# Where the modulation columns of a diffusion trunk are worked out: seven to a head of the linear attention, sixteen beside the output product, few in the up products

## The chip, the cores and the metric

The kernel runs on one core of a Trainium2 chip. The metric is the device time of one execution in microseconds (us). Engines are named as in the profile: PE is TensorE (matrix products), DVE is VectorE, ACT is ScalarE, POOL is GpSimd, and SP (SyncE) issues the DMAs.

## The reference

A diffusion trunk of two layers over 512 tokens of 1024 channels, with a context of 256 tokens:

```python
for l in range(DEPTH):                     # DEPTH = 2
    m = (silu(c) @ ada_w[l] + ada_b[l]).reshape(-1, 6, 1, 1024)      # six modulations
    h = x * (1 + m[:, 1]) + m[:, 0]
    if l % 2 == 0:
        y = even_mixer(h, hc, ...)         # SSD and HGRN2 linear attention, then w_out
    else:
        y = conformer_conv(h, ...)
    x = layer_norm(ALPHA * x + m[:, 2] * y, ...)
    h = x * (1 + m[:, 4]) + m[:, 3]
    u, g = split(h @ w_up)                 # 1024 -> 2 x 2816
    f = (gelu(conv3x3(g)) * u) @ w_down    # 2816 -> 1024
    x = layer_norm(ALPHA * x + m[:, 5] * f, ...)
```

`even_mixer` multiplies h by one wide matrix, runs a state-space scan over 16 heads and a gated linear recurrence (S = diag(f) S + k v, o = S q) over 8 heads in both directions, normalises and gates both results, and multiplies them by `w_out`. Everything is fp32.

A **modulation column** is 128 channels of one of the six modulations of one layer: 8 columns to a modulation, 48 to a layer. The layer's first two modulations of layer 0, for the latent and for the context, are worked out at the start and are 32 columns; 80 columns are left.

## The kernel before

Channels lie on the partitions and tokens along the free axis. fp32 products are made of three matmuls: each operand is split into a high and a low half (hi, lo), and a block is hi x hi + lo x hi + hi x lo (L213 to L215, or L220 to L222 with the activation as the stationary operand). Weights come in loads of four 128 x 128 blocks (256 KB, `wraw`, L181), issued on SP's queue; ACT makes the high half (`whi`, L183) and DVE or POOL the low half (`wlo`, L187): POOL at the start and from the output product on, DVE in between. Six such loads have room.

The stages with their place in the profiled execution:

- start (0 to 110 us) with 32 columns, and the state-space scan (110 to 285);
- linear attention (`gla`, 285 to 640): eight heads, two to a pair. PE makes f, q and v of a head by products of h (`ps`, `psv`, and `psz` for gates). Then seven **levels** follow one another: PE makes four score matmuls (`lev`, L730), DVE merges them into p under a mask (L732), and multiplies the keys and queries `kq` by decays `t` (L734, L736, L738), of which it halves the number for the next level (L740); ACT copies the keys (`kg`, L727). At the end of a head PE transposes keys (`pk`), ACT copies them (`kt`), PE makes `pu`, DVE the states `s` (L755), and PE the output `po`. Products for the next head stand between the levels;
- merge (640 to 682): transposes of y and o (`pt`, L799), the second half of the gate product, and `gate` (L772), which multiplies o by 1/rms (r) and by the gate (sg);
- output product (682 to 755), norm, then the feed-forward part of layer 0: up products with a 3 x 3 convolution on DVE in 22 blocks (up0, 785 to 1030; `acc`, L1021, which reads a product from PSUM, nine taps less one), down products (down0, to 1155);
- layer 1: conformer, up1 (1404 to 1633), down1, output.

A column is one DMA of 512 KB on SP's queue (`ada`, L257), one DVE instruction over 128 x 1024 elements (`junk`, L260) that sums the products of the matrix row and silu(c), and a read of the accumulator (`mod`). Nothing else uses `junk`.

`ada_some(n)` (L264) takes n columns from the list `ada_todo`. It writes them so that they are issued after the instruction in `self.after`, if there is one. The list scheduler that orders each engine's instructions is free to put them later or to move others around them. The columns before are placed so:

- 24 (layer 0, modulations 2, 4 and 3): 8 in merge, 16 behind the output product, with no instruction to come after;
- 56 (layer 0's modulation 5 and all of layer 1): one call in each of the 22 up blocks and calls of 6 in the down products. `self.after` is the last instruction of the norm before (set in `post`) in all of them, and all 56 stand in up0.

The pool `adap` has two buffers for `ada`, so that the third load waits for the first column.

Of the kernel before, what the change touches and what calls it, by code (L numbers as in the profile page):

```python
# [47 lines left out]
GRP = 3  # products that start together after a norm  # L48
NW1, NC1 = 5, 3  # products side by side where the operand comes block by block
# products before a norm that go by halves of the tokens, and for how many of them the weights stay for both halves  # L50
TAIL_W, TAIL_D, TAIL_C = (2, 1), (2, 1), (4, 2)
WB, NWB = 4, 6  # blocks of a load, and loads that have room
# [3 lines left out]
def weight_blocks():  # L56
    """The order in which 128x128 weight blocks are used: (matrix, row, column)."""
# [90 lines left out]
class Net:  # L148
# [28 lines left out]
    def _wload(self):  # L177
# [7 lines left out]
        # by GpSimd where VectorE mostly reads PSUM, which leaves it the port they share  # L185
# [4 lines left out]
    def wblock(self, expect, n=1):  # L190
        """The next n blocks, which lie side by side."""
        while ORDER[self.wpos] is None:
            self.wpos += 1
        p = self.wpos
        assert ORDER[p] == expect, (ORDER[p], expect)
        self.wpos += n
        i, j = divmod(p, WB)
        self.prefetch(i + 1 + self.LA)
        assert j + n <= WB
        hi, lo = self.wtiles[i]  # L200
        return hi[:, j * P:(j + n) * P], lo[:, j * P:(j + n) * P]

    def prefetch(self, upto=None):
        """Weight tiles up to a position, or those of the next products."""
# [5 lines left out]
    def mm3w(self, ps, w, a, start, stop):  # L210
        """ps += w^T a: the weight is the stationary operand."""
# [5 lines left out]
    def mm3a(self, ps, a, w, start, stop):  # L217
        """ps += a^T w: the activation is the stationary operand."""
# [5 lines left out]
    def fm(self, pool, w, col, act, kt=KT, tag="mm", n=T, also=None):  # L224
        """Feature-major product: psum [128 channels, n tokens] (and a second one for `also`)."""
# [14 lines left out]
    def rsqrt(self, y, v, tmp, itmp):  # L240
        """y = v ** -0.5 for small [128, n] tiles: a seed from the exponent, then Newton steps."""
# [9 lines left out]
    def ada(self, layer, j, i, cond=None, out=None, raw=None):  # L251
        """Column of modulation j, channels i*128..: sum_k ada_w[k, ch] silu(c)[k] + ada_b."""
# [6 lines left out]
        junk = self.adap.tile([P, D], BF16, tag="junk", name="junk", bufs=2)  # L259
# [48 lines left out]
    def modulated(self, x, s1, sh, hi, lo, tmp):  # L308
        """hi + lo = x * s1 + sh, split for the tensor engine."""
# [5 lines left out]
    def conv5(self, ps, n, ci, tmps, out=None):  # L315
        """silu of the 5-tap convolution along tokens of a [128, n] psum tile."""
# [12 lines left out]
    def to_tokens(self, src, dst, n, mi):  # L329
        """PE transposes of [128 ch, n*128 tok] into dst [128 tok, n, 128 ch]."""  # L330
# [6 lines left out]
    def mixer(self):  # L337
# [13 lines left out]
        # activations in token blocks as the stationary operand  # L351
# [11 lines left out]
        # startup  # L363
# [8 lines left out]
        with self.pool("pst", 1, PSUM) as pst:  # L372
# [31 lines left out]
            # context modulation, with products of the latent alone meanwhile  # L404
# [19 lines left out]
        self.ada_todo = [(0, j, i) for j in (2, 4, 3) for i in range(8)]  # L424
# [13 lines left out]
        # B of the context  # L438
# [34 lines left out]
        gd = gl.enter_context(self.pool("gla2", 2))  # L473
        for hp in range(4):
# [10 lines left out]
        # gates of the first heads, while the last head's levels follow one another  # L485
# [12 lines left out]
    def dt_stage(self, act, actc, sp, sx, mm, mi, rows):  # L498
# [19 lines left out]
        # softplus = max(x, 0) + 2 atanh(e / (2 + e)), e = exp(-|x|)  # L518
# [21 lines left out]
        # decays: inclusive up to the token, exclusive after it, whole chunks  # L540
# [19 lines left out]
    def zproj(self, i, sz, acth, pool, tag, col=C_Z, dst=None):  # L560
        """silu of 256 channels of a gate, tokens on the partitions."""
# [16 lines left out]
    def ssd(self, g, y, xct, bfm, cfm, btok, dts, rows, sz, sp, tmps, lv, mi):  # L578
# [6 lines left out]
        def bch(t, n):  # [P, GH] -> [P, GH, n] by repetition  # L585
            return bass.AP(tensor=t.tensor, offset=t.offset, ap=[list(t.ap[0]), [1, t.shape[1]], [0, n]])
# [12 lines left out]
        # states: the backward ones for every chunk, the forward one as it goes  # L599
# [12 lines left out]
        # C B^T, transposed: [source, target], cut into the two directions  # L612
# [57 lines left out]
    def gla(self, h, v, act, actc, qs, o, so, gp, gd, mm, lv, mi):  # L670
# [3 lines left out]
        kq = gd.tile([P, 4, T], F32, tag="kq", name="kq")  # K forward, K backward, Q backward, Q forward  # L674
# [13 lines left out]
        # context: keys carried to the end of the context in each direction  # L688
# [24 lines left out]
        # scores inside chunks, target along the free axis: the diagonal, then blocks of 1, 2, .. 64  # L713
# [10 lines left out]
        while m < P:  # L724
# [15 lines left out]
            TT(out=t2, in0=t[:, :, 0::2], in1=t[:, :, 1::2], op=ALU.mult)  # L740
            t, n, m, lev = t2, n // 2, m * 2, lev + 1
        # states at the chunks' starts
# [23 lines left out]

    def gate(self, o, sg, r, h, n):
        """o * r * sg for n heads from h on."""
# [5 lines left out]
    def merge(self, mx, ox, y, o, so, acth):  # L774
# [3 lines left out]
        mp = op.enter_context(self.pool("mop"))  # L778
        ohi = mp.tile([P, 16, T], F32R, name="ohi")
        olo = mp.tile([P, 16, T], F32R, name="olo")  # L780
        ps_ = self.stack()
        self.adap = op.enter_context(self.pool("adap", 2))
# [26 lines left out]
        self.ada_some(8)  # L809
# [10 lines left out]
        # the residual, times alpha, comes back in place of o and stays  # L820
# [10 lines left out]
        bk = [self.mm.tile([P, T], F32, tag="mm", name="psg") for _ in range(NW1)]  # L831
        for k in range(16):
            for i in range(NW1):
                self.mm3w(bk[i], self.wblock(("wout", k * P, i * P)), (ohi[:, k, :], olo[:, k, :]), k == 0, k == 15)
        self.ada_some(99)
# [3 lines left out]
        assert not self.ada_todo  # L839
# [3 lines left out]
        self.ada_todo = [(0, 5, i) for i in range(8)] + [(1, j, i) for j in (2, 1, 0, 4, 3, 5) for i in range(8)]  # L843
        self.post(ln, 0, 0)

# [1 line left out]
    def project(self, ln, w, act, kt, layer, j, tail, then=None, first=0):  # L847
        """x = x + gate * (W^T act), with the norm's sums; the last `tail` blocks go by halves of the tokens."""
# [328 lines left out]
```

## Time and profile before

| | us |
|---|---|
| runs | 1776.51, 1777.94, 1782.64 |
| median | 1777.94 |
| span of the profiled execution, first to last instruction | 1775.1 |
| fastest run over that span | 1.4 |
| linear attention, 285 to 640 | 355 |
| up0, first up matmul to first down matmul | 245.0 |
| up1, the same | 229.0 |

The profile is of one execution. Its span is what the sum is made against; the runs hold a little more than the span. A row of a group of instructions gives the line, engine, operation, tiles and shapes, a count, the busy time and the mean length of one in ns, and behind the last bar the time the engine was idle before them and what it waited for. A row of the timeline gives the start, the length and the same names. An engine's instructions overlap, so the start-to-start distance, not the length, is what a further instruction costs.

### The profile page before, as it was taken

To read this page: it belongs to the slowest core of one execution; us is meant where nothing else is said; L and a number is where in the kernel's file an instruction comes from. 1 tells how busy PE (TensorE), PEld (TensorE's weight loads), DVE (VectorE), ACT (ScalarE), POOL (GpSimd) and SP (SyncE) were. 2 spreads that over 40 slices of the span, in tenths; PEclk is the share of its full clock that TensorE was granted. 3 is DMA by queue.
4 is the path that set the end of the run, shared out by engine and by line. 5 is a ranking of instruction groups with operands and counts; after the bars stand their busy time and mean duration, and the time that the engine had idled before them with its cause. 6 is when DMAs were issued, how large, how long until landed. Compare 5 with 4: busy or idle time off the path is not lost.

```text
span 1775.1 us, 26151 instructions
## 1 busy us (share of the span) xinstructions
PE 1707.4 (96%) x9430; PEld 1457.2 (82%) x9430; DVE 1259.0 (71%) x2384; ACT 845.3 (48%) x1698; POOL 557.3 (31%) x436
## 2 busy tenths in 40 slices
PE   6999999999999999999999999999989999999996
PEld 4987768989999997887777888988869888888886
DVE  6778988857574785589999841478788876776125
ACT  3556775354444544373333332395655744333233
POOL 4400000000000003544566554533414444444451
PEclk9999999999999999999999999999989999999998
DMA  9721001021111147636677433322112333333331
GB/s 344 248 72 48 31 19 53 31 60 36 55 42 54 43 142 259 216 98 200 231 247 246 142 113 96 106 78 60 55 29 78 90 96 100 96 96 99 97 103 64
DMA packets 92195, 194.02 MB, mean 109 GB/s; under 512 B 10497, under 2 KB 13569, under 8 KB 92065
## 3 DMA queue, kind: packets, MB, share of 16 engines
q1 hardware_dynamic: 92016, 192.21, 34.5%
q8 instruction: 74, 1.21, 0.3%
q14 instruction: 57, 0.46, 0.1%
q0 software_dynamic: 48, 0.13, 0.0%
HBM read 190.21 MB, written 2.10 MB: 108 GB/s over the span
## 4 chain that ended last, share of the span: by engine, by line
PE 80%; DVE 15%; DMA 2%; issue 1%; ACT 1%; SPq 0%; POOL 0%; ACTq 0%; POOLq 0%; DVEq 0%
PE ps L213 15%; PE ps L215 15%; PE ps L214 15%; DVE acc L1021 4%; DVE junk L260 4%; PE lev L730 3%; PE psg L214 2%; PE psg L213 2%; PE psg L215 2%; PE psh L214 2%; PE psh L213 2%; PE psh L215 2%; PE seg L631 2%; PE psz L221 1%; PE psz L220 1%; PE psz L222 1%
## 5 line engine op out<-in xcount | busy, mean ns | idle before, releaser
L187 POOL TENSOR_TENSOR wlo<-wraw,whi 128x512 fp32r<-128x512 f32 x388 | 541.4, 1403 | 1172.3 <-ACT whi L183 1153.2
L183 ACT CAST whi<-wraw 128x512 fp32r<-128x512 f32 x488 | 298.1, 618 | 418.8 <-PE ps L214 214.5
L213 PE MATMUL ps<-h1hi,whi 128*128 128x512 f32 x760 | 297.9, 392 | 12.1 <-DVE acc L1021 12.0
L215 PE MATMUL ps<-h1hi,wlo 128*128 128x512 f32 x760 | 297.1, 391 | 0.3 <-POOL wlo L187 0.2
L214 PE MATMUL ps<-h1lo,whi 128*128 128x512 f32 x760 | 296.7, 390 | 0.0
L1021 DVE SCALAR_TENSOR_TENSOR acc<-ps,pcol,acc 128x441 f32<-128x441 f32 (+2 forms) x320 | 216.9, 691 | 34.8 <-ACT acc L1013 28.6
L213 PEld LDWEIGHTS ps<-h1hi,whi 128*128 128x128 f32 x760 | 143.1, 188 | 45.6 <-issue 16.9
L215 PEld LDWEIGHTS ps<-h1hi,wlo 128*128 128x128 f32 x760 | 143.1, 188 | 30.8 <-POOL wlo L187 1.2
L214 PEld LDWEIGHTS ps<-h1lo,whi 128*128 128x128 f32 x760 | 143.3, 188 | 29.1
L260 DVE CUSTOM_DVE_ANT_0 junk<-ada,sc,pcol 128x1024 bf16<-128x1024 f32 x80 | 113.3, 1419 | 27.4 <-DMA ada<-adaw 27.4
L872 DVE SCALAR_TENSOR_TENSOR x<-ps,mod,x 128x512 f32<-128x512 f32 x14 | 10.5, 750 | 148.9 <-PE ps L215 148.9
L187 DVE TENSOR_TENSOR wlo<-wraw,whi 128x512 fp32r<-128x512 f32 x100 | 68.9, 693 | 53.0 <-ACT whi L183 45.9
L1098 DVE SCALAR_TENSOR_TENSOR cr<-u,pcol,cr 128x256 f32<-128x256 f32 (+24 forms) x172 | 104.6, 682 | 1.4 <-ACT cr L1077 1.2
L215 PE MATMUL ps<-ghi,wlo 128*128 128x512 f32 x264 | 102.8, 389 | 0.0
L213 PE MATMUL ps<-ghi,whi 128*128 128x512 f32 x264 | 102.8, 389 | 0.0
L214 PE MATMUL ps<-glo,whi 128*128 128x512 f32 x264 | 102.8, 389 | 0.0
L213 PE MATMUL ps<-hhi,whi 128*128 128x512 f32 x240 | 98.2, 409 | 0.0
L1023 ACT ACTIVATE acc<-acc 128x512 f32<-128x512 f32 x44 | 27.7, 632 | 145.0 <-DVE acc L1021 145.0
L215 PE MATMUL ps<-hhi,wlo 128*128 128x512 f32 x240 | 96.1, 400 | 0.0
L214 PE MATMUL ps<-hlo,whi 128*128 128x512 f32 x240 | 95.8, 399 | 0.0
L939 DVE TENSOR_TENSOR glo<-acc,ghi 128x512 fp32r<-128x512 f32 x44 | 61.4, 1397 | 18.6 <-ACT ghi L938 18.4
L222 PE MATMUL psz<-whi,hlo 128*128 128x256 f32 (+1 forms) x224 | 67.6, 302 | 0.0
(366 smaller groups left out, 4167.1 us busy)
## 6 DMA issues: line engine op xcount, KB each, us to landing
wraw<-wst SPq DMA_DIRECT2D x488, 256.0 KB, 2.7
ada<-adaw SPq DMA_DIRECT2D x104, 512.0 KB, 4.1
xk<-xT SPq DMA_DIRECT2D x8, 256.0 KB, 7.8
x<-xT SPq DMA_DIRECT2D x8, 256.0 KB, 4.8
out<-n SPq DMA_DIRECT2D x16, 128.0 KB, 1.7
xk<-ctxT SPq DMA_DIRECT2D x8, 128.0 KB, 4.4
sc<-rows SPq DMA_DIRECT2D x1, 512.0 KB, 4.4
scc<-rows SPq DMA_DIRECT2D x1, 512.0 KB, 7.6
```

Source lines behind the costliest of these rows:

```text
L183: nc.scalar.copy(hi, raw)
L187: eng.tensor_tensor(out=lo, in0=raw, in1=hi.bitcast(F32), op=ALU.subtract)
L213: mm(ps, w[0], a[0], start=start, stop=False)
L214: mm(ps, w[0], a[1], start=False, stop=False)
L215: mm(ps, w[1], a[0], start=False, stop=stop)
L222: mm(ps, a[1], w[0], start=False, stop=stop)
L260: nc.vector.tensor_tensor_reduce(out=junk, in0=raw, in1=self.sc if cond is None else cond, scale=1.0, scalar=self.pc("adab", n), op0=ALU.m ...
L631: nc.tensor.matmul(seg, (self.gt, self.lt)[d], r[:, d], start=d == 0, stop=d == 1)
L730: nc.tensor.matmul(ps[:, c, :], kg[:, c * P:(c + 1) * P], ap(kq, 2 * T + c * P, [[2 * m, P // (2 * m)], [T + m, 2], [1, m]]), start=True, ...
L939: nc.vector.tensor_tensor(out=lo, in0=x, in1=hi.bitcast(F32), op=ALU.subtract)
L1021: nc.vector.scalar_tensor_tensor(out=o, in0=grid(pg)[:, r0 + dy - 1:r1 + dy - 1, c0 + dx - 1:c1 + dx - 1], scalar=wcol(dy, dx), in1=o, op0 ...
L1098: nc.vector.scalar_tensor_tensor(out=acc[:, t0:t1], in0=u[:, t0 + d:t1 + d], scalar=self.pc("cdw", tap * 8 + i), in1=acc[:, t0:t1], op0=AL ...
```

## The change

There is one list of 80 columns, and it is given out earlier. `gla` gives out one column behind each level's last multiplication (`ADA_HEAD` = 7, so at all seven levels), to be issued after that multiplication: 56 columns. 16 more (`ADA_OUT`) are asked for ahead of the output product, to be issued after the last head's last such multiplication. Eight are left for the feed-forward part of layer 0: one in every fourth up block (6, after that block's split) and 2 in the first down product. Layer 1 works out none, as before. `junk` has one buffer and not two, and `adap` is opened in the attention, and in merge ahead of `ohi`. `residual` and `split` now hand out their instruction for `self.after`. The comments are taken out, which moves line numbers by 1 to 6.

```diff
-        junk = self.adap.tile([P, D], BF16, tag="junk", name="junk", bufs=2)
+        junk = self.adap.tile([P, D], BF16, tag="junk", name="junk", bufs=1)
...
-        self.ada_todo = [(0, j, i) for j in (2, 4, 3) for i in range(8)]
+        self.ada_todo = [(l, j, i) for l, js in ((0, (2, 4, 3, 5)), (1, (2, 1, 0, 4, 3, 5))) for j in js for i in range(8)]
...
         gd = gl.enter_context(self.pool("gla2", 2))
+        self.adap = gl.enter_context(self.pool("adap", 2))
...
-            TT(out=t2, in0=t[:, :, 0::2], in1=t[:, :, 1::2], op=ALU.mult)
+            self.after = TT(out=t2, in0=t[:, :, 0::2], in1=t[:, :, 1::2], op=ALU.mult)
+            if lev < self.ADA_HEAD:
+                self.ada_some(1)
             t, n, m, lev = t2, n // 2, m * 2, lev + 1
...
+    ADA_HEAD, ADA_OUT, ADA_DOWN = 7, 16, 5
...
         mp = op.enter_context(self.pool("mop"))
+        self.adap = op.enter_context(self.pool("adap", 2))
         ohi = mp.tile([P, 16, T], F32R, name="ohi")
         olo = mp.tile([P, 16, T], F32R, name="olo")
         ps_ = self.stack()
-        self.adap = op.enter_context(self.pool("adap", 2))
...
         emit(o, "hnw", 0, 8)
-        self.ada_some(8)
...
+        self.ada_some(self.ADA_OUT)
         for k in range(16):
             for i in range(NW1):
                 self.mm3w(bk[i], self.wblock(("wout", k * P, i * P)), (ohi[:, k, :], olo[:, k, :]), k == 0, k == 15)
-        self.ada_some(99)
...
-        assert not self.ada_todo
...
-        self.ada_todo = [(0, 5, i) for i in range(8)] + [(1, j, i) for j in (2, 1, 0, 4, 3, 5) for i in range(8)]
...
-            self.split(acc, ghi[:, i, :], glo[:, i, :])
+            self.after = self.split(acc, ghi[:, i, :], glo[:, i, :])
...
-            self.ada_some(1)
+            if layer == DEPTH - 1 or i % 4 == 0:
+                self.ada_some(1)
...
-        self.project(ln, f"dn{layer}", lambda k: (ghi[:, k, :], glo[:, k, :]), FT, layer, 5, TAIL_D, lambda i: self.ada_some(6))
+        self.project(ln, f"dn{layer}", lambda k: (ghi[:, k, :], glo[:, k, :]), FT, layer, 5, TAIL_D, lambda i: self.ada_some(0 if layer or i > 3 else self.ADA_DOWN))
```

What it makes of the order is seen at three places. In rows of the order, a column is `ISA junk,mod<-ada,sc,pcol` and the `ISA mod` behind it.

DVE in the levels of a head of the attention, before (two levels of the fourth head):

```order
L732 COPY_PREDICATED p<-msk,lev 128x512
L736 TENSOR_TENSOR kq<-kq,t 128x32x8
L738 TENSOR_TENSOR kq<-kq,t 128x32x8
L734 TENSOR_TENSOR kq<-kq,t 128x2x8x32
L732 COPY_PREDICATED p<-msk,lev 128x512
L736 TENSOR_TENSOR kq<-kq,t 128x16x16
L738 TENSOR_TENSOR kq<-kq,t 128x16x16
```

The same in the changed kernel (L732 to L740 are L733 to L741 there):

```order
L733 COPY_PREDICATED p<-msk,lev 128x512
L735 TENSOR_TENSOR kq<-kq,t 128x2x8x32
L737 TENSOR_TENSOR kq<-kq,t 128x8x32
L739 TENSOR_TENSOR kq<-kq,t 128x8x32
L741 TENSOR_TENSOR t<-t 128x16
L260 ISA junk,mod<-ada_4587,sc,pcol 128x1024
L260 ISA mod 128x1
L733 COPY_PREDICATED p<-msk,lev 128x512
```

The wide multiplication (L734, L735), which stood last in a level, now stands right behind p; t, which had been made ahead, stands in its level, and a column behind it.

PE behind the last level of the last head, before (`psz` is a gate's product, which the scheduler puts between):

```order
L730 MATMUL lev<-kq,kg 128x128 x4
L748 MATMUL pk<-tri,kq 128x128 x3
L222 MATMUL psz<-whi_6010,hlo 128x256
L220 MATMUL psz<-whi_6010,hhi 128x256
L221 MATMUL psz<-wlo_6012,hhi 128x256
L222 MATMUL psz<-whi_6010,hlo 128x256
L220 MATMUL psz<-whi_6070,hhi 128x256
L753 MATMUL pu<-v,kt 128x128 x3
```

And now:

```order
L731 MATMUL lev<-kq,kg 128x128 x4
L751 MATMUL pk<-tri,kq 128x128 x3
L756 MATMUL pu<-v,kt 128x128 x3
L751 MATMUL pk<-tri,kq 128x128 x3
L756 MATMUL pu<-v,kt 128x128 x3
L221 MATMUL psz<-wlo_6563,hhi 128x256
```

No product stands between the transposes and `pu` any more, and the first product behind them reads `wlo_6563`. On DVE that low half stands behind the last column of the head:

```order
L733 COPY_PREDICATED p<-msk,lev 128x512
L735 TENSOR_TENSOR kq<-kq,t 128x2x4x64
L737 TENSOR_TENSOR kq<-kq,t 128x4x64
L739 TENSOR_TENSOR kq<-kq,t 128x4x64
L741 TENSOR_TENSOR t<-t 128x8
L260 ISA junk,mod<-ada_6494,sc,pcol 128x1024
L260 ISA mod 128x1
L758 SCALAR_TENSOR_TENSOR s<-s,t,pu 128x128
L246 TENSOR_TENSOR t<-r 128x16
L187 TENSOR_TENSOR wlo_6563<-wraw_6559,whi_6561 128x512
```

DVE in merge, between the two multiplications of the gate, in the changed kernel (o x r, then o x sg):

```order
L778 TENSOR_TENSOR o<-o,r 128x4x128
L260 ISA junk,mod<-ada_7181,sc,pcol 128x1024
L260 ISA mod 128x1
L260 ISA junk,mod<-ada_7185,sc,pcol 128x1024
L260 ISA mod 128x1
L187 TENSOR_TENSOR wlo_7057<-wraw_7053,whi_7055 128x512
L187 TENSOR_TENSOR wlo_7075<-wraw_7071,whi_7073 128x512
L260 ISA junk,mod<-ada_7189,sc,pcol 128x1024
L260 ISA mod 128x1
L260 ISA junk,mod<-ada_7193,sc,pcol 128x1024
L260 ISA mod 128x1
L778 TENSOR_TENSOR o<-o,sg 128x4x128 x4
```

These are four of the sixteen columns asked for ahead of the output product; three more stand ahead of o x r, nine behind o x sg. In up0, where 56 columns stood between the convolution's steps, six are left.

More of the change, by code (lines that the diff above doesn't have):

```diff
@@ L871, in residual @@
         r = self.x[:, i, t0:t1]
-        self.nc.vector.scalar_tensor_tensor(out=r, in0=ps, scalar=self.modc(layer, j, i), in1=r, op0=ALU.mult, op1=ALU.add)
+        self.after = self.nc.vector.scalar_tensor_tensor(out=r, in0=ps, scalar=self.modc(layer, j, i), in1=r, op0=ALU.mult, op1=ALU.add)
         return self.x[:, i, :]
@@ L938, in split @@
         nc.scalar.copy(hi, x)
-        nc.vector.tensor_tensor(out=lo, in0=x, in1=hi.bitcast(F32), op=ALU.subtract)
+        return nc.vector.tensor_tensor(out=lo, in0=x, in1=hi.bitcast(F32), op=ALU.subtract)
     def post(self, ln, layer, which):
```

## The prediction

> **What bounds the kernel now.** I read the first part of the page, then the chain that ended last, then the stages side by side.
>
> ```profile
> span 1775.1 us, 26151 instructions
> PE 1707.4 (96%) x9430; PEld 1457.2 (82%) x9430; DVE 1259.0 (71%) x2384; ACT 845.3 (48%) x1698; POOL 557.3 (31%) x436
> PE 80%; DVE 15%; DMA 2%; issue 1%; ACT 1%; SPq 0%; POOL 0%; ACTq 0%; POOLq 0%; DVEq 0%
> ```
>
> TensorE is busy almost throughout, so no column costs time by itself. It costs time where it makes VectorE late for something that TensorE waits for. The windows, one row per stage (linear attention, merge, output product, up0, up1), show where VectorE has no room:
>
> ```profile
> 285.00:640.00 355.00, 354.90 (x2452) 325.60 (x2451) 233.99 (x568) 163.05 (x337) 0.00 (x0) 1.00 0.17 49
> 640.00:682.00 42.00, 38.80 (x209) 32.69 (x208) 37.99 (x68) 20.83 (x34) 3.36 (x2) 0.96 0.62 211
> 682.00:755.00 73.00, 73.00 (x373) 62.57 (x372) 36.60 (x57) 25.19 (x43) 39.94 (x28) 1.00 0.73 239
> 785.00:1030.00 245.00, 232.89 (x1028) 190.07 (x1027) 235.02 (x341) 94.33 (x163) 140.62 (x86) 0.99 0.63 206
> 1404.00:1633.00 229.00, 228.66 (x1027) 189.86 (x1027) 164.79 (x228) 99.77 (x163) 111.54 (x87) 1.00 0.34 99
> ```
>
> After the length come PE, PEld, DVE, ACT and POOL busy, then the granted clock, the DMA share and GB/s. VectorE is busy for 235 of 245 us in up0, for 165 of 229 in up1 (the same work for layer 1) and for 234 of 355 in the attention. TensorE is full in the attention and loses 12 us in up0.
>
> **The 48 columns that leave up0 (and 2 of its 8 others).** up0 and up1 issue the same 328 x 3 wide matmuls, so one prices the other. Their limits are the first up matmul and the first down matmul:
>
> ```profile
> L213 PE MATMUL ps<-h1hi,whi x333: 388/390/629, 784.7 to 1179.8; 128*128 128x512 f32 x167
> L213 PE MATMUL ps<-ghi,whi x132: 388/389/390, 1029.7 to 1118.8; 128*128 128x512 f32 x132
> L213 PE MATMUL ps<-h1hi,whi x328: 388/389/467, 1403.6 to 1631.9; 128*128 128x512 f32 x164
> L213 PE MATMUL ps<-ghi,whi x132: 388/389/390, 1632.6 to 1721.7; 128*128 128x512 f32 x132
> ```
>
> up0 takes 1029.7 - 784.7 = 245.0 us, up1 takes 1632.6 - 1403.6 = 229.0, 16.0 less. What up0 has beside up1 is this, and what TensorE waits for there follows it:
>
> ```profile
> L260 DVE CUSTOM_DVE_ANT_0 junk<-ada,sc,pcol 128x1024 bf16<-128x1024 f32 x56 | 82.0, 1466 | 0.0
> PE ps L213 <- DVE acc L1021: 11.8, 9, 2.3
> 800.83 0.39 PE L215 MATMUL ps<-h1hi,wlo 128*128 128x512 f32 x1
> 803.52 0.47 PE L213 MATMUL ps<-h1hi,whi 128*128 128x512 f32 x1 [2.31 <-DVE acc L1021]
> 804.81 0.63 PE L214 MATMUL ps<-h1lo,whi 128*128 128x512 f32 x1
> ```
>
> The 56 columns fill VectorE (82.0 us), the convolution's steps (L1021) free the PSUM banks late, and TensorE waits nine times, 11.8 us. The rest of the 16 is matmuls at half rate behind the longest wait (0.43 us from start to start at 804.81, 0.23 before it) and short gaps. [...]
>
> Afterwards six columns are left, one to every fourth block: 6 x 1.47 = 9 us of VectorE, against 229 - 165 = 64 us of idle time that up1 has. Their operands have two buffers and come long ahead. So up0 becomes up1: **-16.0**, with ends -17 and -14. The two in down0 are 2.9 us of VectorE at the most, beside 132 x 3 matmuls (89 us) that read only finished operands: 0.
>
> **The 56 columns that enter the attention.** One costs 1.22 us of VectorE from start to next start where no GpSimd work runs beside it (649.40 to 650.62):
>
> ```profile
> 649.40 1.28 DVE L260 CUSTOM_DVE_ANT_0 junk<-ada,sc,pcol 128x1024 bf16<-128x1024 f32 x1
> 650.62 0.08 DVE L260 DVE_READ_ACCUMULATOR2_ANT mod<- 128x1 f32 x1
> 650.62 2.06 DVE L803 SCALAR_TENSOR_TENSOR olo<-pt,pcol,ohi 128x512 fp32r<-128x512 f32 x3
> ```
>
> That is 56 x 1.22 = 68 us: VectorE goes from 234 to 302 of 355 us, 85%. By share it fits, as a sum. The question is order, since the levels of a head form a chain between TensorE (lev) and VectorE (p, then kq three times). Two levels before:
>
> ```profile
> 437.05 0.41 DVE L738 TENSOR_TENSOR kq<-kq,t 128x256 f32<-128x256 f32 x1
> 437.39 0.68 DVE L734 TENSOR_TENSOR kq<-kq,t 128x512 f32<-128x512 f32 x1
> 438.78 0.75 DVE L732 COPY_PREDICATED p<-msk,lev 128x512 f32<-128x512 int32 x1 [0.71 <-PE lev L730]
> 439.42 0.41 DVE L736 TENSOR_TENSOR kq<-kq,t 128x256 f32<-128x256 f32 x1
> 439.74 0.42 DVE L738 TENSOR_TENSOR kq<-kq,t 128x256 f32<-128x256 f32 x1
> 440.08 0.69 DVE L734 TENSOR_TENSOR kq<-kq,t 128x512 f32<-128x512 f32 x1
> 441.47 0.74 DVE L732 COPY_PREDICATED p<-msk,lev 128x512 f32<-128x512 int32 x1 [0.71 <-PE lev L730]
> 437.61 1.13 PE L730 MATMUL lev<-kq,kg 128*128 128x128 f32 x8
> 438.50 0.36 PE L222 MATMUL psv<-whi,hlo 128*128 128x256 f32 x1
> 440.31 1.13 PE L730 MATMUL lev<-kq,kg 128*128 128x128 f32 x8
> ```
>
> A level takes 441.47 - 438.78 = 2.69 us: p 0.64, two kq 0.32 + 0.34, L734 in the shadow of TensorE, and 0.71 of waiting. Between two lev groups (0.89 us) TensorE has 440.31 - 438.50 = 1.8 us of product matmuls. In the changed order the big kq stands right behind p, and t and the column stand in the shadow. The period by the same rows is then p 0.64 + kq 0.60 + kq 0.33 + 1.73 from the last kq to the next p (438.78 - 437.05) = 3.30 us, and in the 1.73 stand the last kq (0.33), t (0.1 to 0.3) and the column (1.22), which just fill it. TensorE therefore needs 3.30 - 0.89 = 2.4 us of product matmuls between lev groups. Counting those that stand there now, at the trace's 0.23 us (512 wide) and 0.12 us (256 wide), I get 2.0 to 3.4 us for most levels: it mostly balances, with nothing in hand.
>
> The small steps that the walk through a head needs, besides:
>
> ```profile
> L755 DVE SCALAR_TENSOR_TENSOR s<-s,t,pu 128x128 f32<-128x128 f32 x48 | 16.6, 347 | 6.3 <-PE pu L753 5.3
> L740 DVE TENSOR_TENSOR t<-t 128x256 f32<-128x256 f32 (+5 forms) x48 | 11.6, 241 | 0.3
> L187 DVE TENSOR_TENSOR wlo<-wraw,whi 128x512 fp32r<-128x512 f32 x62 | 42.7, 691 | 44.3 <-ACT whi L183 37.5 <-issue 6.5
> ```
>
> Walking through the heads with these durations, TensorE is short by about 0.15 us at the second level, 0.35 at the last and 0.45 where po waits for s: about 1.0 in each of the four heads that begin a pair, and 0.5 in the other three, 5.5 together. The last head is dearer. Behind its last lev group stand only pk, pu, pk, pu (1.0 us) and then psz on a weight whose low half VectorE makes behind p, three kq, t, the column and one s. From the start of lev that is 1.07 to p, 0.64 + 0.60 + 0.33 + 0.33 + 0.1, the column's 1.22, the s (0.35) and 0.7 for the low half: 5.4 us, against 0.9 + 1.0 of TensorE work, 3.4 us idle, and about 1 us of half rate behind it as at 804.81. Sum: 5.5 + 3.4 + 1 = **+10**. The lower bound is 0 (all of it hides, as 34% of VectorE's time would allow), the upper the whole lengthening of the chain, 56 x (3.30 - 2.69) = 34. I stay near the low end since the row of the attention shows a full TensorE with work to put between; for the likeliest case 3 to 16.
>
> The columns' loads share SyncE's queue with the weights, and each waits for the column two before it. In up0 such a load takes 3.6 us to land, about the 3.3 us of a level, and there are two buffers:
>
> ```profile
> ada<-adaw SPq DMA_DIRECT2D x54, 512.0 KB, 3.6
> SPq L257 <- DVE mod L260: 95.1, 50, 4.3
> PE ps L215 <- POOL wlo L187: 0.2, 1, 0.2
> ```
>
> The waiting loads hold weight loads behind them (95.1 us of that in up0, where a weight's low half was late once, by 0.2), and in the new order those weights are first used some 20 us on: 0.
>
> **Merge and output product.** The only long stall of TensorE there waits for the gated o:
>
> ```profile
> 671.58 0.39 PE L215 MATMUL psg<-ohi,wlo 128*128 128x512 f32 x1
> 675.16 1.94 PE L799 MATMUL pt<-tri,o 128*128 128x128 f32 x8 [3.20 <-DVE o L772]
> 672.06 2.35 DVE L772 TENSOR_TENSOR o<-o,r 128x512 f32<-128x512 f32 x2
> 674.34 1.88 DVE L772 TENSOR_TENSOR o<-o,sg 128x512 f32<-128x512 f32 x3
> ```
>
> Eight columns stood ahead of o x sg before; now seven do, three ahead of o x r and four behind it, the last two held by loads that start only as two others end. With 3.6 us to a landing I get o x sg at about 672 to 674 in the old time against 674.34. The TensorE order around the transposes is the same. I take **-1**, between -4.5 (the 3.2 go, and the slowing behind it, 1.3 us by the granted clock: 0.96 over 42 us against 0.99 in up0) and +2 (one load more late). The nine behind it stand beside a product with no gap, where 16 stood: 0.
>
> **Sum.** -16 + 10 - 1 = -7 us. Span 1775.1 becomes 1768; the fastest run (1776.51) lies 1.4 us over the span, the median 1777.94 by 2.8, so against the median 1777.94 - 7 = **1771**. The runs spread by about 0.3%, 5.3 us: faster is below 1772.6, slower above 1783.3.
>
> **Rivals.**
> - Everything hides in the attention, by its 34% of idle VectorE time, and merge's stall shrinks too: -16 + 1 - 2 = -17, 1761. Against it stands the last head, whose TensorE order has nothing left to put between.
> - The level chain pays. VectorE takes its instructions in order, so a column in front of p delays it, and with a period of 3.30 no level has room for a late copy or load. If TensorE lacks matmuls at every level, 34 us come, -16 + 34 - 1 = +17, 1795. It decides once the attention loses more than 22 us, 2.8 per head or 0.4 per level, two thirds of the lengthening of 0.61. Against it: 44 us of TensorE work per head, 7 x 3.3 = 23 of chain. [...]
> - The columns don't stay where they were written: those of the output product have already moved ahead of o x sg. If their loads come late by 2 us twice, merge gets +4 instead of -1, and 1776 follows, within 0.3%.
> - Weights come late behind the columns' loads: a clump of loads waits through some levels, and a stall of 1 us per pair of heads or two gives +4 to +8, 1775 to 1779.
>
> **How the numbers follow.** All hidden: 0.12. My forecast, attention +3 to +16: 0.58, of which 0.45 falls under +12 and so below 1772.6. A loss of 16 to 22, or the third or fourth rival on top: 0.15. The chain pays: 0.15. Faster 0.57, same 0.28, slower 0.15. The likeliest case's own range is 1764 to 1777; with the other cases on both sides 1761 to 1783.
>
> **What would show it.** up0 should last 229 to 231 us with waits on acc under 1 us and no half rate. Attention: lev to lev 3.3 us in place of 2.7, VectorE 300 us busy, TensorE gaps of 0.3 to 0.5 us at last levels and one of about 3.4 us at the last head's end, before psz. Merge: the wait on o below 3.2. I am wrong if the attention lengthens by over 16 us or under 3, above all by gaps at every p, or if TensorE there waits on weights.

## The result, and the profile after

The changed kernel takes 1765.2 us (median of 4 runs, 1763.29 to 1765.97) against 1778.4 before: a ratio of 0.9919, 95% interval 0.9903 to 0.9935. Measured again beside other kernels it took 1766.8 us (six runs, 1762.8 to 1769.6) against 1779.6, ratio 0.9922 [0.9907, 0.9938]. It is 13 us faster; 7 were forecast, within a range of 1761 to 1783.

The first part of the page after, and its chain that ended last:

```profile
span 1762.9 us, 26221 instructions
PE 1705.8 (97%) x9430; PEld 1457.4 (83%) x9430; DVE 1250.0 (71%) x2384; ACT 850.0 (48%) x1698; POOL 525.8 (30%) x436
PE 89%; DVE 6%; ACT 1%; issue 1%; DMA 0%; POOL 0%; ACTq 0%; DVEq 0%; POOLq 0%
```

VectorE's part of the chain falls from 15% to 6%, and no row of the columns (L260) is left among the chain's dearest. The windows of the attention and of up0, columns as before:

```profile
282.60:645.90 363.30, 360.71 (x2476) 330.09 (x2475) 296.17 (x683) 164.02 (x340) 0.00 (x0) 0.99 0.40 129
789.40:1018.60 229.20, 228.62 (x1028) 189.58 (x1027) 173.13 (x246) 100.15 (x162) 113.14 (x87) 1.00 0.38 113
```

The starts of the same matmuls in the changed kernel, for up0, and what TensorE still waits for there:

```profile
L213 PE MATMUL ps<-h1hi,whi x336: 389/389/467, 789.4 to 1169.9; 128*128 128x512 f32 x168
L213 PE MATMUL ps<-ghi,whi x132: 389/389/389, 1018.6 to 1107.7; 128*128 128x512 f32 x132
  DVE acc L1024: 0.4, 1
```

up0 lasts 1018.6 - 789.4 = 229.2 us, as up1 does, and the waits on acc go from 11.8 us to 0.4. For the attention, the first lev from kq and kg and the first transpose of y; these two rows give its length in all the runs below:

```profile
L731 PE MATMUL lev<-kq,kg x448: 270/275/377, 298.8 to 625.2; 128*128 128x128 f32 x150
L805 PE MATMUL pt<-tri,y x32: 270/273/329, 645.9 to 652.9; 128*128 128x128 f32 x32
```

That is 347.1 us against 642.9 - 301.2 = 341.7 before. The levels run as the arithmetic had them (VectorE's timeline, two levels of one head):

```profile
433.61 0.75 DVE L733 COPY_PREDICATED p<-msk,lev 128x512 f32<-128x512 int32 x1 [0.21 <-PE lev L731]
434.25 0.68 DVE L735 TENSOR_TENSOR kq<-kq,t 128x512 f32<-128x512 f32 x1
...
435.65 1.28 DVE L260 CUSTOM_DVE_ANT_0 junk<-ada,sc,pcol 128x1024 bf16<-128x1024 f32 x1
436.90 0.74 DVE L733 COPY_PREDICATED p<-msk,lev 128x512 f32<-128x512 int32 x1
440.20 0.75 DVE L733 COPY_PREDICATED p<-msk,lev 128x512 f32<-128x512 int32 x1
```

From p to p it is 3.29 and 3.30 us. Yet TensorE hardly waits. I count each matmul from start to start against 0.11, 0.12 and 0.23 us for 128, 256 and 512 columns, their pace in this trace where nothing waits (eight of lev in 1.05 us at 400.55, the last of them 0.27; psz from 619.81 to 619.93; ps from 399.64 to 399.87): up to the last head's last level it loses no more than 0.20 us at any one place, and the losses of 0.15 us and more sum to 0.9 us there, against 1.5 in the whole attention before. The loss is in one place:

```profile
624.27 1.16 PE L731 MATMUL lev<-kq,kg 128*128 128x128 f32 x8
626.82 0.55 PE L751 MATMUL pk<-tri,kq 128*128 128x128 f32 x3 [1.39 <-DVE kq L735]
627.93 1.45 PE L756 MATMUL pu<-v,kt 128*128 128x128 f32 x6 [0.57 <-ACT kt L753]
629.17 0.85 PE L751 MATMUL pk<-tri,kq 128*128 128x128 f32 x3
630.59 1.65 PE L756 MATMUL pu<-v,kt 128*128 128x128 f32 x6 [0.57 <-ACT kt L753]
631.89 0.56 PE L221 MATMUL psz<-wlo,hhi 128*128 128x256 f32 x1
...
627.43 1.28 DVE L260 CUSTOM_DVE_ANT_0 junk<-ada,sc,pcol 128x1024 bf16<-128x1024 f32 x1
629.77 0.69 DVE L187 TENSOR_TENSOR wlo<-wraw,whi 128x512 fp32r<-128x512 f32 x1
```

Start to start, beyond the matmuls' own time at full rate, these steps lose 1.65 + 0.77 + 0.57 + 1.08 + 0.62 + 0.24 = 4.9 us, and the products behind them go at half rate for a while (granted clock 0.50 from 628.2 to 635.0, 0.21 us from start to start for 256 columns).

In merge TensorE waits for the gated o as long as before, 3.02 us against 3.20, but for another reason:

```profile
671.59 2.64 ACT L818 ACTIVATE sg<-psz 128x512 f32<-128x512 f32 x4
672.53 1.29 DVE L260 CUSTOM_DVE_ANT_0 junk<-ada,sc,pcol 128x1024 bf16<-128x1024 f32 x1 [0.27 <-DMA ada<-adaw]
675.27 1.93 DVE L260 CUSTOM_DVE_ANT_0 junk<-ada,sc,pcol 128x1024 bf16<-128x1024 f32 x1 [1.45 <-DMA ada<-adaw]
677.14 2.49 DVE L778 TENSOR_TENSOR o<-o,sg 128x512 f32<-128x512 f32 x4
677.96 0.63 PE L805 MATMUL pt<-tri,o 128*128 128x128 f32 x4 [3.02 <-DVE o L778]
...
680.72 0.63 PE L213 MATMUL psg<-ohi,whi 128*128 128x512 f32 x1
681.14 0.63 PE L214 MATMUL psg<-olo,whi 128*128 128x512 f32 x1
```

Two columns in front of o x sg wait for their loads (0.27 and 1.45 us). VectorE took them in the order that the change gave it: sg was ready at 671.59 + 2.64 = 674.23, and o x sg began at 677.14, behind the second column. Behind the wait the matmuls go at half rate (0.42 us from start to start, 680.72 to 681.14, against 0.23 ahead of it; granted clock 0.50 from 679.4 to 682.8).

By stages, each from such first starts, in us (the attention ends with the first transpose of y, merge with the first matmul of the output product, the next with the last of its first five columns; "norm" holds the rest of the product and the norm):

| | start | attention | merge | five products | norm | up0 | down0 | conformer | up1 | end |
|---|---|---|---|---|---|---|---|---|---|---|
| before | 301.2 | 341.7 | 27.5 | 60.3 | 54.0 | 245.0 | 89.8 | 284.1 | 229.0 | 142.5 |
| changed | 298.8 | 347.1 | 27.5 | 60.5 | 55.5 | 229.2 | 89.8 | 282.7 | 229.1 | 142.7 |
| changed, again | 300.0 | 347.2 | 27.5 | 60.5 | 56.9 | 229.2 | 89.8 | 285.0 | 229.0 | 142.8 |

The two profiles of the changed kernel differ by 5 us in start, norm and conformer, and agree to 0.1 everywhere else. What the change does is +5.4 in the attention, -15.8 in up0 and +0.2 beside. That is -10.2; the other 3 us of the medians lie in no stage of these profiles. The execution of before that was profiled was among its fastest (span 1775.1, the median run 1778 to 1780).

Norm and conformer scatter with the granted clock. These are the windows of norm before, in the changed kernel and in the changed kernel again:

```profile
730.70:784.70 54.00, 50.43 (x371) 47.65 (x370) 39.51 (x95) 28.14 (x53) 26.53 (x18) 1.00 0.37 110
733.90:789.40 55.50, 51.90 (x370) 49.12 (x369) 41.77 (x95) 28.12 (x53) 23.71 (x18) 0.97 0.30 86
735.10:792.00 56.90, 53.31 (x371) 50.60 (x370) 41.86 (x95) 28.13 (x53) 23.66 (x19) 0.94 0.29 84
```

The clock of 0.97 is one stretch at 0.50, from 764.7 to 768.1; the 0.94 stands for twice that by my estimate (0.06 x 56.9 / 0.5 = 6.8 us), and 1.00 for none. Each stretch makes norm 1.4 to 1.5 us longer. In the conformer the changed kernel has 17 us at half rate in the profile of 282.7 us (1290.4 to 1293.8, 1314.3 to 1324.5, 1365.5 to 1368.9) and 24 us in that of 285.0, whose clock over the whole span is 0.984 against 0.987; the kernel before has 24 us and 284.1. So two executions of one program differ by this. That the other 3 us of the medians are such scatter is likely, but no run here shows it.

### The profile page after: what moved, and what is told of

Its sections match the earlier page's. It is cut to its first block, busy times and chain, and to the rows that moved or that the text cites. A ratio compares the mean times of both kernels' runs of the same rounds, so it can differ in the third digit from the quotient of the medians.

```text
span 1762.9 us, 26221 instructions
## 1 busy us (share of the span) xinstructions
PE 1705.8 (97%) x9430; PEld 1457.4 (83%) x9430; DVE 1250.0 (71%) x2384; ACT 850.0 (48%) x1698; POOL 525.8 (30%) x436
## 4 chain that ended last, share of the span: by engine, by line
PE 89%; DVE 6%; ACT 1%; issue 1%; DMA 0%; POOL 0%; ACTq 0%; DVEq 0%; POOLq 0%
PE ps L213 18%; PE ps L215 18%; PE ps L214 18%; PE lev L731 3%; PE psg L214 2%; PE psh L213 2%; PE psh L214 2%; PE psh L215 2%; PE psg L215 2%; PE psg L213 2%; PE seg L632 2%; PE psz L221 1%; PE psz L222 1%; PE psz L220 1%; PE psv L221 1%; PE psv L222 1%
## 5 line engine op out<-in xcount | busy, mean ns | idle before, releaser
L187 POOL TENSOR_TENSOR wlo<-wraw,whi 128x512 fp32r<-128x512 f32 x388 | 510.0, 1318 | 1191.6 <-DMA wraw<-wst 596.0
L1024 DVE SCALAR_TENSOR_TENSOR acc<-ps,pcol,acc 128x441 f32<-128x441 f32 (+2 forms) x320 | 222.4, 695 | 58.0 <-ACT acc L1016 48.5
L215 PEld LDWEIGHTS ps<-h1hi,wlo 128*128 128x128 f32 x760 | 142.7, 188 | 30.7 <-POOL wlo L187 1.2
L213 PEld LDWEIGHTS ps<-h1hi,whi 128*128 128x128 f32 x760 | 142.7, 188 | 30.5 <-issue 1.4
L214 PEld LDWEIGHTS ps<-h1lo,whi 128*128 128x128 f32 x760 | 142.7, 188 | 29.2
L260 DVE CUSTOM_DVE_ANT_0 junk<-ada,sc,pcol 128x1024 bf16<-128x1024 f32 x80 | 105.4, 1317 | 17.2 <-DMA ada<-adaw 17.1
L942 DVE TENSOR_TENSOR glo<-acc,ghi 128x512 fp32r<-128x512 f32 x44 | 56.1, 1274 | 28.3 <-ACT ghi L941 28.1
L220 PE MATMUL psz<-whi,hhi 128*128 128x256 f32 (+1 forms) x224 | 67.9, 304 | 0.0
L221 PE MATMUL psz<-wlo,hhi 128*128 128x256 f32 (+1 forms) x224 | 67.7, 303 | 0.0
```

Of the source, the lines that this page charges most:

```text
L187: eng.tensor_tensor(out=lo, in0=raw, in1=hi.bitcast(F32), op=ALU.subtract)
L213: mm(ps, w[0], a[0], start=start, stop=False)
L214: mm(ps, w[0], a[1], start=False, stop=False)
L215: mm(ps, w[1], a[0], start=False, stop=stop)
L220: mm(ps, a[0], w[0], start=start, stop=False)
L221: mm(ps, a[0], w[1], start=False, stop=False)
```

## Experiments

**The attention without its columns, and with the last head free.** The first kernel leaves the 56 columns of the attention out, load and sum, so that its output is not the reference's:

```diff
             if lev < self.ADA_HEAD:
-                self.ada_some(1)
+                self.ada_todo.pop(0)
```

> The changed kernel with the attention's 56 columns left out altogether (neither load nor sum; the modulation is set to zero once instead, so the output is not the reference's). Theory A: the columns in the attention cost only what stands at the last head, 5.2 us of TensorE gaps, and nothing at the other seven. Then the attention falls from 348.0 us (first lev to first pt) to 342.6 to 343, and the kernel from 1765.2 to about 1760. Rival B: the columns hide entirely and the 5.4 us are the run's own scatter: 1765. Rival C: they also load the DMA queue and the weights, and more than 5.4 comes back: below 1758.

The attention took 341.6 us, the kernel 1762.9 (1761.7 to 1763.5), ratio 0.9904 [0.9891, 0.9917]. The attention's 5.5 us are the columns', as theory A had it; the total fell by less than its 5 us, start and conformer being 2 to 3 us longer in this profile.

The second keeps 49 columns there and takes out the last head's seven:

```diff
-            if lev < self.ADA_HEAD:
+            if h < 7 and lev < self.ADA_HEAD:
...
-            if layer == DEPTH - 1 or i % 4 == 0:
+            if layer == DEPTH - 1 or i % 2 == 0:
```

> The changed kernel with the last head's seven columns taken out of the attention: 11 columns in up0 (every second block) and 4 in down0 in place of 6 and 2. Theory A: products stand again between the last head's transposes, its gaps of 5.2 us fall below 0.7, up0 stays at 229 to 230 us since VectorE has 64 us to spare there against 11 x 1.4 = 15; 1760. Rival B: the gap is the tail of any head without a successor and stays: 1765. Rival C: up0 pays for 5 columns more in proportion to before, 16.0/56 = 0.29 us each, 1.4: 1761.5.

1761.0 us (1760.0 to 1763.7), ratio 0.9897 [0.9884, 0.9909]. The attention's window:

```profile
299.30:640.90 341.60, 341.53 (x2378) 312.86 (x2377) 278.87 (x644) 154.38 (x323) 0.00 (x0) 1.00 0.37 118
```

With 49 columns in it and VectorE 279 us busy it lasts 341.6 us, as with none: seven heads pay nothing, the last one everything. up0 stays at 229.2 with 11 columns.

**Which columns of the last head.** Its last three levels alone, then its first four alone (`h < 7 or lev >= 4`, `h < 7 or lev < 4`, the others in up0):

> The changed kernel with the last head's columns at its last three levels alone (the first four moved to up0). What makes the last head dear: theory A1, its chain is longer at every level (0.7 us each of the 5.2) and no later head lends products; then three columns cost about 2.2 us, the attention is at 343.8. Theory A2, only what stands behind the last lev group matters, the column in front of the states and of the low half that the next product reads; then nearly all of it is here, 346 to 347.

> The changed kernel with the last head's columns at its first four levels alone (the last three moved to up0). Theory A1: four columns cost 4 x 0.7 = 2.9 us, the attention is at 344.5. Theory A2: no column stands behind the last three lev groups, so nothing is lost: 341.6 to 342.

Both gave 341.3 us of attention, in one run each (1763.7 and 1763.8 us in all); the first of the two:

```profile
L731 PE MATMUL lev<-kq,kg x448: 270/275/378, 300.1 to 625.0; 128*128 128x128 f32 x150
L805 PE MATMUL pt<-tri,y x32: 272/273/328, 641.4 to 648.4; 128*128 128x128 f32 x32
```

Both theories miss: three columns at the end cost nothing, nor do four at the start, and seven cost 5.4. It is a threshold, not a price by the column and not the place of the last one. In both kernels products stand between the last head's transposes, in the changed kernel none: its longer levels have used up the products whose weights were ready. Counted in the traces, the gate product has 192 matmuls in the attention. Ahead of the last lev group TensorE has issued 86 of them in the kernel before, 99 and 105 in these two, and 110 in the changed kernel.

**Twice the VectorE time.** Each of the 56 sums is run twice on the same block:

```diff
-                    self.ada(*self.ada_todo.pop(0))
+                    l, j, i = self.ada_todo.pop(0)
+                    raw = self.ada(l, j, i)
+                    if twice:
+                        self.ada(l, j, i, raw=raw)
```

> The changed kernel with each of the attention's 56 sums run twice on the same loaded block (the load once): twice the VectorE time, the same transfers. Theory A: VectorE's whole time decides. 234 + 2 x 68 = 371 us is over the 342 of TensorE's work, so VectorE becomes the bound and the attention lasts 375 to 385 us, 1795 to 1803 in all. Rival B: the chain of each level decides, 3.30 + 1.22 = 4.5 us, and products fill it: about 7 x 4.5 = 32 of 43 us per head, no loss but at the last head, whose tail grows by 7 x 1.2: 356 us, 1775.

1849.4 us (one run); the attention 430.7 us (lev from 299.0 to the first transpose of y at 729.7), 84 more than the changed kernel. Both theories are far too low. The window from 298 to 733 us has VectorE busy for 82% of it, so it isn't simply full:

```profile
298.00:733.00 435.00, 383.39 (x2408) 345.78 (x2407) 357.87 (x778) 159.31 (x329) 0.00 (x0) 0.89 0.32 103
PE pk L754 <- DVE kq L738: 20.7, 8, 2.6
PE lev L734 <- DVE t L744: 15.7, 8, 3.4
PE pu L759 <- ACT kt L756: 9.1, 16, 0.6
```

The wait in front of pk, which the changed kernel has once, now comes eight times, once a head, with the granted clock at 0.89. Every head has become a last head: its levels took the products, and its tail stood open. The waits in front of pk and pu sum to 29.8 us; the 15.7 us in front of lev are the levels' own chain, which now stops TensorE too, and much of the rest is matmuls at the lower clock. That the first column of a level cost nothing in seven heads and the second 84/56 = 1.5 us on average, more than its own 1.22, fits the same threshold, seen from the other side.

**The low halves on GpSimd.** If the low half of the next product's weight is what is late, GpSimd, idle in the attention, can make it:

```diff
         r = self.rstd(gp, so[:, 0:4 * NCH], 4 * NCH, P)
+        self.lo_pool = True
         for q in range(2):
...
             self.gate(o, sg, r, 2 * q, 2)
+        self.lo_pool = False
```

> The changed kernel, all seven columns of the last head in place, with one edit: the low halves of the eight loads behind the attention (the gates' weights, wlo_6563 first) are made by GpSimd, which is idle there, and not by VectorE. Theory A: the last head's gap is the low half that waits on VectorE behind the chain and two columns (its high half was ready at 623.7 us, the low half began at 629.8); then the gap closes, psz stands between pk and pu, and the attention falls from 347.1 to 341.3 to 342.5 with no column moved. Rival B: the chain itself is too long for what products are left: 345 or more. Rival C: GpSimd's reads slow VectorE's instructions, as up0 shows (1466 against 1278 ns for a column): 343 to 345.

1770.9 us (1769.6 to 1771.8), ratio 0.9948 [0.9928, 0.9967], no gain over the changed kernel's 0.9919 and 0.9922; the attention 347.5, merge 29.0, where it had 347.1 and 27.5. The products do stand between the transposes now, but a new gap has opened ahead of them:

```profile
622.02 6.68 POOL L187 TENSOR_TENSOR wlo<-wraw,whi 128x512 fp32r<-128x512 f32 x4 [15.69 <-ACT whi L183]
622.33 1.28 DVE L743 TENSOR_TENSOR t<-t 128x32 f32<-128x32 f32 x1
623.53 2.36 DVE L260 CUSTOM_DVE_ANT_0 junk<-ada,sc,pcol 128x1024 bf16<-128x1024 f32 x1
627.50 1.49 DVE L739 TENSOR_TENSOR kq<-kq,t 128x256 f32<-128x256 f32 x1
629.47 1.34 PE L733 MATMUL lev<-kq,kg 128*128 128x128 f32 x6 [3.40 <-DVE t L743]
```

While GpSimd makes four low halves, a column takes 2.36 us in place of 1.28, a kq 1.49 in place of 0.42, and the chain is 3.4 us late. Rival C, larger than expected. The changed kernel has the same in merge: its column at 675.27 takes 1.93 us, with a low half of GpSimd running from 674.86 to 676.12, where the 56 columns of the attention, with GpSimd idle, take 1.28 on average. Each of the two instructions here is roughly 1.1 us longer, and one low half takes GpSimd 6.68 / 4 = 1.7 us; what the two engines share is not shown by any run.

The tail itself has closed. From the start of the last lev group to the first transpose of y it is 17.4 us here, against 21.6 in the changed kernel and 17.5 before, as theory A had it. But the last lev group begins 4.6 us later than in the changed kernel, counted from the first one, and that delay gave the low halves time as well. So whether the low half alone made the last head's gap stays open.

**The output product's columns behind the gate.**

```diff
-        self.gate(o, sg, r, 4, 4)
+        self.after = self.gate(o, sg, r, 4, 4)
```

(`gate` returns its last multiplication.)

> The changed kernel with the 16 columns of the output product held back until the gate's last multiplication. Theory A: o x sg waited for two columns whose loads stood behind weight loads (the last one landed 1.45 us late); with none ahead it starts when sg is there, about 674.3 in the changed kernel's time in place of 677.1, TensorE's wait of 3.02 us falls to 0.3 or less and the half rate behind it (1.3 us) goes: -3 to -4.3, about 1761.5. Rival B: 16 columns paced by their loads at 2.75 us each reach to 720 and further and hold the first residual, at 734: no gain, 1765 or more. Rival C: the weights' low halves of the output product stand behind the columns on VectorE and come late: slower than 1766.

The five products took 57.5 us in place of 60.5, and o x sg now waits for sg, not for a load:

```profile
675.81 3.58 DVE L778 TENSOR_TENSOR o<-o,sg 128x512 f32<-128x512 f32 x4 [2.00 <-ACT sg L819]
676.65 1.23 PE L806 MATMUL pt<-tri,o 128*128 128x128 f32 x8 [0.60 <-DVE o L778]
```

The stage is theory A's, -3.0, and no later wait took its place. The total, 1764.8 us (1761.6 to 1768.0), ratio 0.9916 [0.9902, 0.9929], does not show it beyond its scatter.

**Both edits.** The last head free, and the 16 behind the gate:

> The changed kernel with both edits: the last head's seven columns in up0 and down0, and the 16 of the output product held back until the gate's last multiplication. Theory A: the two gains stand at different places and add up, the attention 347.1 to 341.6 and the first five output products 60.5 to 57.5, 8.5 us less than the changed kernel, 1756 to 1757. Rival B: with o x sg early, the 16 columns and their loads collide with the output product's weights: the second gain is lost, 1760.

1760.3 us (1758.7 to 1761.8) against 1766.8 for the changed kernel on the same chip, ratio to before 0.9890 [0.9876, 0.9904]: the lowest time here, though the last head's edit alone, at 0.9897 [0.9884, 0.9909], can't be told from it. The stages are as expected: attention 341.6, five products 57.6. With the last head free alone the five products had come down to 58.8 already, so beside that edit the gate's is worth 1.2 us there and not 3. The total is 3 to 4 us higher than expected; 1.6 of it is that the 1765.2 that I counted from lies below the 1766.8 measured here.

**Pool low halves and gate together**, from the low halves' edit:

> The same, with the 16 columns of the output product held back until the gate's last multiplication. The gains add up as they did with the last head's columns moved: attention 341.3 to 342.5, the first five output products 57.5, 1758 to 1760.5 in all, the same as that kernel (1760.3) within 0.1%. Rival: the low halves of the gate's weights, made by GpSimd at 1.3 us in place of 0.7, come late for the gate product, and merge grows from 27.5 by 1 or more.

1767.2 us (1765.7 to 1770.2), ratio 0.9931 [0.9908, 0.9954]; five products 57.5, but attention 348.3 and merge 29.0: the rival, and VectorE's longer instructions beside GpSimd with it.

**How many columns up0 can hold.** First the kernel before with only the anchors: a column is held behind its block's split, so that 22 stand in up0 and 34 in down0.

```diff
-            self.split(acc, ghi[:, i, :], glo[:, i, :])
+            self.after = self.split(acc, ghi[:, i, :], glo[:, i, :])
```

(and the same for `residual`)

> The kernel before with one thing of the change: the columns of the up blocks are held behind that block's split, and those of the down products behind that product's residual, so that 22 stand in up0 and 34 in down0. Nothing enters the attention. Theory A: the 16.0 us of up0 come from 56 columns in 245 us; 22 make 165 + 32 = 197 us of VectorE in 229, so up0 falls to 229 to 231 us, down0 hides 34 columns (48 us of VectorE that waits there), and the kernel is at 1778.4 - 15.5 = 1763, a little under the changed kernel, without a column in the attention. Rival B: each column costs up0 its 0.29 us: 6 us are left, 1769. Rival C: the columns' loads, six in a row, hold the down product's weights or residuals, and down0 lengthens by more than 3 us: 1766 or more.

up0 fell to 229.2 us, as theory A had it, but the kernel took 1786.9 (1781.3 to 1791.4), ratio 1.0044 [1.0032, 1.0056], slower than before. Rival C, larger than it was put: down0 and what follows lost 4 + 15 us. The last of TensorE's waits there, and SyncE's queue in down0:

```profile
1128.90 0.58 PE L213 MATMUL psh<-ghi,whi 128*128 128x256 f32 x1 [7.22 <-ACT whi L183]
SPq L257 <- DVE mod L260: 58.6, 32, 4.7
```

From 1053 us on the columns' loads and the weight loads take turns in SyncE's queue. Each column's load waits for the column two before, and the weight load behind it comes late; TensorE stands for 7.2 us. That is the fourth rival of the prediction, at a place where it did not stand.

Then 40 in up0, two to a block in 18 blocks:

```diff
-    ADA_HEAD, ADA_OUT, ADA_DOWN = 7, 16, 5
+    ADA_HEAD, ADA_OUT, ADA_DOWN = 3, 16, 5
...
-            if layer == DEPTH - 1 or i % 4 == 0:
-                self.ada_some(1)
+            if layer == 0:
+                self.ada_some(2 if i < 18 else 1)
```

> The changed kernel with columns at the first three levels of each head alone (24) and 40 in up0: two in each of 18 blocks, one in four, each held behind its block's split; none in down0. Theory A: up0 loses time only when VectorE is full: 165 + 40 x 1.4 = 221 of 229 us is not, so up0 stays at 229 to 232; the attention is at 341.6 to 343.5; 1761 to 1764 in all. Rival B: each column costs up0 the 0.29 us of the kernel before: 229 + 11.6 = 241, 1772. Rival C: two columns in a row behind a split hold the next block's convolution by 2.8 us, more than the PSUM banks have in hand: 229 + 18 x 0.5 = 238.

1778.2 us (1774.3 to 1783.6), ratio 0.9994 [0.9980, 1.0008]: up0 239.6 us, and down0 5.5 longer, since its first blocks wait for the last of acc. Theory A falls: VectorE was busy for only 212 of 240 us there, and yet TensorE waited for it. One block of its timeline shows how:

```profile
949.77 0.69 DVE L1027 TENSOR_TENSOR acc<-acc,ps 128x512 f32<-128x512 f32 x1 [0.76 <-ACT acc L1026]
950.96 0.68 DVE L1024 SCALAR_TENSOR_TENSOR acc<-ps,pcol,acc 128x441 f32<-128x441 f32 x1 [0.50 <-ACT acc L1016]
951.56 0.68 DVE L942 TENSOR_TENSOR glo<-acc,ghi 128x512 fp32r<-128x512 f32 x1
952.16 2.32 DVE L260 CUSTOM_DVE_ANT_0 junk<-ada,sc,pcol 128x1024 bf16<-128x1024 f32 x1
954.40 0.67 DVE L1024 SCALAR_TENSOR_TENSOR acc<-ps,pcol,acc 128x448 f32<-128x448 f32 x1
955.00 1.70 DVE L260 CUSTOM_DVE_ANT_0 junk<-ada,sc,pcol 128x1024 bf16<-128x1024 f32 x1
```

From start to next start the two columns take 2.24 + 1.64 = 3.9 us beside GpSimd's low halves (GpSimd is busy for 130 of the 230 us from 780 to 1010), not 2 x 1.22, and the waits on ScalarE stay. From 913.2 us on TensorE's waits on acc come 12.0 us apart (nine, of 0.82 to 0.86 us), while a block's 48 matmuls take 48 x 0.227 = 10.9: one us a block. Before that there is a single one, 0.42 us at 803.2, so some blocks went by on the PSUM tiles in hand, as I read it:

```profile
PE ps L213 <- DVE acc L1024: 8.0, 10, 0.9
```

The 10.4 us are near rivals B (11.6) and C (9). But B's price per column is refuted by the run before this, where 22 columns cost nothing. The 40 stood in pairs behind a split; 40 placed otherwise were not run.

## Why the prediction was right

**up0, -16.0.** Right: -15.8. Pricing it by its twin in layer 1 held to 0.2 us. Its reason, a full VectorE, holds as far as that few columns are free (6, 11, 22); that any number is free until VectorE is busy all the time is wrong, as 40 in pairs showed.

**Attention, +10.** The place was right and the sum was off by half: +5.4. The period of a level was 3.30 us, as worked out. The term that failed is the 5.5 us of short stalls in the first seven heads (0.15 + 0.35 + 0.45 in a head): they did not come, and no place there loses more than 0.20 us. The likely reason is that the walk charged every lateness of a few tenths to TensorE while products stood next in its order. The last head was put at 3.4 + 1 and measured 5.4, at the place named, with psz behind pk, pu, pk, pu on `wlo_6563`. Its product began 7.6 us behind the start of the last lev group (631.89 - 624.27); 5.4 had been put, since I let the copies of pk hide. The wait that was named for it is not in the trace. The low half was ready at 629.77 + 0.69 = 630.46, 1.4 us before that product; TensorE waited for kq in front of the first pk (1.39) and for ACT's copies in front of each pu (0.57 twice). That 3.4 + 1 lies near 5.4 is in part luck.

**Merge, -1.** The step that failed is the landing of the last two loads. I had o x sg at 672 to 674 of the old time; it came at 677.1, merge having begun 3 us later, so at 674.1. The gain was nothing, and the experiment behind the gate shows that 3.0 us were there to be had.

**The rivals.** "Everything hides" was nearer than I gave it credit for (0.12): in 49 of 56 columns it is so. The level chain did not pay at one column a level, and with two it did at once, so the balance had as little in hand as said. SyncE's queue made no weight late in the changed kernel's attention (the columns' loads waited there for 195.9 us in 53 waits, and TensorE's waits, 1.4 and 1.1 us, are on kq and kt), and did where columns' loads and weight loads took turns in down0, with the 7.22 us of TensorE; in merge it is the columns' own loads that came late, by 0.27 and 1.45 us. The half rate came again behind the wait on o, 3.02 us, with matmuls at 0.43 us from start to start in place of 0.23. In the last head the clock fell to 0.50 (628.2 to 635.0) though no single wait was longer than 1.39 us.

**The total.** -7 against -13: 4.6 us from the attention's term, partly offset by 1 in merge, and about 3 that no stage of the profiles holds. The range of 22 us was wide enough to hold all of this; the stages bear out more of the prediction than the total does.

## What to carry to other kernels

Price a stage that is overloaded by a twin of it that isn't, if the program has one; here that gave the largest term to 0.2 us. When side work goes into a chain between two engines, work out the chain's new period, and then ask how much independent work is left to fill it: up to that amount the side work was free here, beyond it a piece cost more than its own length (1.5 us for 1.22), and the last pass of a loop, with no successor to lend work, crosses the line first. Loads that waited for their consumers held the weight loads behind them in SyncE's queue in down0 (58.6 us of waits there, 7.2 us of TensorE), so keep such loads out of the way of loads that matter.

## What the hardware showed that was not expected

Beside GpSimd's low halves VectorE's instructions took far longer than the average seen in up0 (1466 against 1278 ns): a single column took 2.36 us, and a 128 x 32 step 1.28 us in place of 0.18. Moving work to an idle GpSimd made the chain on VectorE later by 3.4 us here.
